# Mamba-2 inside a chunk: the values as weights, the decays moving, and a transpose back

## The chip, the cores and the metric

The kernel runs on one core of a Trainium2 chip. The metric is the device time of one execution in microseconds (us). TensorE (PE in the rows) multiplies, with its weight loads shown as an engine of their own (PEld); VectorE (DVE), ScalarE (ACT) and GpSimd (POOL) do the element-wise work; SyncE (SP) and ACT issue the DMAs.

## What is computed

One layer of a bidirectional encoder over 1024 tokens: a norm, one wide input projection, three recurrent branches (RWKV-7, HGRN2 and Mamba-2, called SSD), their gated sum, an output projection and an FFN. The change lies in the SSD branch. Cut to what matters, for each chunk of 128 tokens, 16 heads of 64 values, 2 groups of 8 heads:

```python
cb = jnp.einsum('bcqgn,bcsgn->bcqsg', cm, bm)
y_diag = jnp.einsum('bcqsgh,bcsghp->bcqghp', cb[..., None] * lmat, xdt)   # inside a chunk
...
y_off = jnp.einsum('bcqgn,bcghpn->bcqghp', cm, prev) * jnp.exp(a_cum)[..., None]
return (y_diag + y_off).reshape(b, L, H, P)
y = y_f + y_b + xs * d_skip[:, None]          # both directions and the skip
```

`y_diag` is the part in question: a 128x128 matrix per head and chunk (decays times scores) against 128x64 values.

## The kernel before

Everything is one instruction stream per engine. A scheduler that simulates the kernel sets the order on PE, DVE, ACT and SP; only POOL's order in the chunk loop is written by hand (`manual_schedule`). Products in full float32 run as two passes, so that eight matmuls show as 16 records; the wide products use float32r and one pass each.

`ssd` (L1204) handles the two groups of 8 heads one after the other. For a group it convolves the inputs (`conv`), transposes the values into token rows `xt` (L1347), and then runs the **chunk loop** (L1381), eight iterations. Iteration i works on chunk i in the forward direction (d=0) and on chunk 7-i in the backward one (d=1). In each direction:

- `yo` (L1391) multiplies by the state `S[d]`; DVE scales it to `yt` (L1393); POOL adds it to the accumulator `Y` (L1394).
- `xw` (L1397, DVE) and `st` (L1399, PE) give the state's update; POOL decays `S` (L1403), DVE adds (L1404; in the first iteration a copy, L1401).

`pairs(c)` (L1361) prepares the 128x128 matrices `E` of a later chunk: two DMAs broadcast the cumulated decays (L1367), POOL subtracts (L1370, twice), DVE picks the halves (L1373), ACT takes the exponential (L1374), DVE multiplies by the scores `CB` (L1375). The `E` buffers rotate, five in all. In iterations 0 to 3 POOL also starts two rows of `Y` from the skip (L1384).

At the end of iteration i stands the product `yd`: for each head, `E` as weights (128x128) and the head's 64 columns of `xt` moving, into one PSUM bank of token rows (128 x 512), which DVE adds to `Y[:, i]` (L1412).

Between these steps the kernel hands out **job matmuls**: the input projection of branches that come later, 3696 matmuls of 128x128 by 128x512 at L330 to L332, cut into pieces by `J.share` (L354). They keep PE busy while the chunk loop waits. Every job loads its weights (ACT cast `wh`, L221; DVE remainder `wl`, L223) and has its result copied out by ACT (`st`, L272) and stored. After the loop, `Y` is transposed into channel rows (`ytps`, L1430). When the second group is done, the branches are merged (`merges`, L1474), for which the last job results are loaded back (`gt`).

Of the kernel before, what the change touches and what calls it, by code (L numbers as in the profile page):

```python
# [9 lines left out]
F32 = mybir.dt.float32  # L10
# [8 lines left out]
P = 128  # L19
# [7 lines left out]
DECAY = 0.6065306597  # L27
NORM_EPS = 1e-6
EB = 5
TB = 6  # L30
PE = mybir.EngineType.PE
ACT = mybir.EngineType.Activation
# [967 lines left out]
def hgrn(g):  # L1000
# [3 lines left out]
    with ExitStack() as es:  # L1004
# [4 lines left out]
        def tl(tag, shape=(P, L), bufs=1, dt=F32):  # L1009
            return hp.tile(list(shape), dt, tag=tag, name=tag, bufs=bufs)  # L1010

        def gates(hd):

            kf = [tl("kf", bufs=2), tl("kb", bufs=2)]
            gg = tl("gg", bufs=2)
            sg = tl("t", bufs=TB)
            for d in range(2):
# [39 lines left out]
        def front(hd):  # L1057
# [4 lines left out]
            nc.sync.dma_start(fr.q, J.get(g.ph, hd))  # L1062
            lf = [tl("t", bufs=TB), tl("t", bufs=TB)]
            fr.cm = [tl("cf"), tl("cb")]
# [13 lines left out]
            fr.scd = tl("scd", (P, NT, 64))  # L1078
            ks = tl("t", bufs=TB)
            nc.vector.tensor_add(ks, kf[0], kf[1])  # L1080
# [11 lines left out]
        for hd in range(4):  # L1092
            fr = nxt
            q, gg, cm, scd = fr.q, fr.gg, fr.cm, fr.scd
            iv = tl("t", bufs=TB)
            nc.sync.dma_start(iv, J.get(g.ph, 12 + hd))
            Vt = tl("Vt", (P, NT, P))

            def transp(dst, src):
                for h in range(2):  # L1100
                    ps = pp.tile([P, 4, P], F32, tag="a", name="tps", bufs=4)
                    for j in range(4):
                        t = h * 4 + j
                        nc.tensor.transpose(ps[:, j], src[:, t * P:(t + 1) * P], g.ident)
                    nc.scalar.copy(dst[:, h * 4:h * 4 + 4], ps)
# [14 lines left out]
            for d in range(2):  # L1120
                c3, ck3 = (t.rearrange("p (c t) -> p c t", t=P) for t in (cm[d], fr.ck[d]))
                last = (P - 1) if d == 0 else 0
                kd = tl("t", bufs=TB)
                kd3 = kd.rearrange("p (c t) -> p c t", t=P)
# [5 lines left out]
            for d in range(2):  # L1130
                kt = tl("t", (P, NT, P), bufs=TB)
                transp(kt, kds[d])
# [71 lines left out]
def ssd(g, xr):  # L1204
    nc, tc, A, J = g.nc, g.tc, g.A, g.J
# [7 lines left out]
    with ExitStack() as es:  # L1213
        kp = es.enter_context(tc.tile_pool(name="s0", bufs=1))
        pp = es.enter_context(tc.tile_pool(name="s0ps", bufs=1, space=PSUM))
# [13 lines left out]
        with tc.tile_pool(name="s0t", bufs=1) as tp:  # L1229
# [15 lines left out]
            for src, dst in ((dt, dtT), (dA, dAT)):  # L1245
                ps = pp.tile([P, NT, 32], F32, tag="a", name="dtps", bufs=3)
# [43 lines left out]
        def conv(ct, dst):  # L1290

            pt = sp.tile([P, L + 4], F32, tag="E", name="pt", bufs=EB)
            nc.gpsimd.memset(pt[:, 0:2], 0.0)
            nc.gpsimd.memset(pt[:, L + 2:L + 4], 0.0)
            nc.sync.dma_start(pt[:, 2:L + 2], J.get(g.px, ct))
            w = V["conv_w"]
            acc = sp.tile([P, L + 4], F32, tag="E", name="acc", bufs=EB)[:, :L]
            nc.scalar.activation(acc, pt[:, 0:L], AF.Identity, scale=w[:, ct:ct + 1], bias=V["conv_b"][:, ct:ct + 1])
            for k in range(1, 5):
                nc.vector.scalar_tensor_tensor(acc, pt[:, k:k + L], w[:, k * 12 + ct:k * 12 + ct + 1], acc,  # L1300
                                               MUL, ADD)
            nc.scalar.activation(dst, acc, AF.Silu)
# [3 lines left out]
        yp = es.enter_context(tc.tile_pool(name="s1y", bufs=1))  # L1306
        sp = es.enter_context(tc.tile_pool(name="s1", bufs=1))
        for grp in range(2):
            with ExitStack() as es2:
                xt = ep.tile([P, NT, 512], F32, tag="xt", name="xt")  # L1310
# [9 lines left out]
                for h in range(2):  # L1320
                    ps = pp.tile([P, 4, P], F32, tag="a", name="cbps", bufs=3)
# [17 lines left out]
                for q in range(4):  # L1339
                    xq = sp.tile([P, L + 4], F32, tag="E", name="xq", bufs=EB)[:, :L]  # L1340
                    conv(grp * 4 + q, xq)
                    J.share(F[2])
                    for h in range(2):
                        ps = pp.tile([P, 4, P], F32, tag="a", name="xps", bufs=3)
# [5 lines left out]
                Y = yp.tile([P, NT, 512], F32, tag="Y", name="Y")  # L1350

                def per_head(tab, c, d):
                    return tab[:, c, d * 16 + grp * 8:d * 16 + grp * 8 + 8].unsqueeze(2).broadcast_to([P, 8, 64])

                def h3(t):
                    return t.rearrange("p (h v) -> p h v", v=64)
# [4 lines left out]
                def pairs(c):  # L1361

                    Es = []
                    for d in range(2):
                        e = sp.tile([P, L + 4], F32, tag="E", name="E", bufs=EB)
                        e = e[:, :L].rearrange("p (h t) -> p h t", t=P)
                        nc.sync.dma_start(e, cumd[d * 16 + grp * 8:d * 16 + grp * 8 + 8, c * P:(c + 1) * P]  # L1367
                                          .unsqueeze(0).broadcast_to([P, 8, P]))
                        cs = cums[:, c, d * 16 + grp * 8:d * 16 + grp * 8 + 8]
                        nc.gpsimd.tensor_tensor(e, e, cs.unsqueeze(2).broadcast_to([P, 8, P]), SUB)  # L1370
                        Es.append(e)
                    e = Es[0]
                    nc.vector.copy_predicated(e, m8.unsqueeze(1).broadcast_to([P, 8, P]), Es[1])  # L1373
                    nc.scalar.activation(e, e, AF.Exp)  # L1374
                    nc.vector.tensor_mul(e, e, CB[:, c:c + 1, :].broadcast_to([P, 8, P]))  # L1375
                    return e
# [4 lines left out]
                for i in range(NT):  # L1381
                    if i < NT // 2:
                        for c in (i, NT - 1 - i):
                            nc.gpsimd.tensor_tensor(h3(Y[:, c]), h3(xt[:, c]),  # L1384
                                                    gd[:, c].unsqueeze(2).broadcast_to([P, 8, 64]), MUL)
                    e = nxt.pop(0)
                    for d in range(2):
                        c = i if d == 0 else NT - 1 - i
                        if i > 0:
                            ps = pp.tile([P, 512], F32, tag="b", name="yo", bufs=2)  # L1390
                            nc.tensor.matmul(ps, CT[:, c * P:(c + 1) * P], S[d], start=True, stop=True)  # L1391
                            yt = yp.tile([P, 512], F32, tag="yt", name="yt", bufs=2)
                            nc.vector.tensor_tensor(h3(yt), h3(ps), per_head(ecum, c, d), MUL)  # L1393
                            nc.gpsimd.tensor_add(Y[:, c], Y[:, c], yt)  # L1394
                        if i < NT - 1:
                            xw = yp.tile([P, 512], F32, tag="xw", name="xw", bufs=2)
                            nc.vector.tensor_tensor(h3(xw), h3(xt[:, c]), per_head(wst, c, d), MUL)  # L1397
                            ps = pp.tile([P, 512], F32, tag="b", name="st", bufs=2)
                            nc.tensor.matmul(ps, Bt[:, c], xw, start=True, stop=True)  # L1399
                            if i == 0:  # L1400
                                nc.vector.tensor_copy(S[d], ps)  # L1401
                            else:
                                nc.gpsimd.tensor_tensor(h3(S[d]), h3(S[d]), per_head(dec, c, d), MUL)  # L1403
                                nc.vector.tensor_add(S[d], S[d], ps)  # L1404
                        if d == 0 and i + 2 < NT:
                            nxt.append(pairs(i + 2))
                        J.share(F[4])
                    ps = pp.tile([P, 8, 64], F32, tag="a", name="yd", bufs=3)
                    for h in range(8):
                        nc.tensor.matmul(ps[:, h], e[:, h], xt[:, i, h * 64:h * 64 + 64],  # L1410
                                         start=True, stop=True)
                    nc.vector.tensor_add(Y[:, i], Y[:, i], ps.rearrange("p h v -> p (h v)"))  # L1412
                    J.share(F[5])
                order.close()
                if grp == 1:
                    xr.load(*range(4))
                zss = []
                for q in range(4):
                    zs = sp.tile([P, L + 4], F32, tag="E", name="zs", bufs=EB)[:, :L]
                    nc.sync.dma_start(zs, J.get(g.pz, grp * 4 + q))  # L1420
# [4 lines left out]
                for q in range(4):  # L1425
                    zs = zss[q]
                    for h in range(2):
                        ps = pp.tile([P, 4, P], F32, tag="a", name="ytps", bufs=3)
# [7 lines left out]
                    else:  # L1436
                        sq = sp.tile([P, L + 4], F32, tag="E", name="sq", bufs=EB)[:, :L]
                        nc.scalar.activation(sq, zs, AF.Square)
# [593 lines left out]
def layer_kernel(ctx, tc, A, out):  # L2032
# [27 lines left out]
    g.gtp = ctx.enter_context(tc.tile_pool(name="gtp", bufs=1))  # L2060
    xr = Operand(g, r, (0,))
    ysc, ss = ssd(g, xr)
    rg = ExitStack()
    ring = [rg.enter_context(tc.tile_pool(name=f"ring{i}", bufs=1)) for i in range(2)]
# [72 lines left out]
```

## Time and profile before

| | |
|---|---|
| time, median of 3 runs | 2425.1 us (2421.72 to 2426.01) |
| the profiled execution | 2419.83 us, its span 2418.1 us |
| PE busy | 2276.5 us, 94% |
| DVE, POOL, ACT busy | 1568.5 (65%), 1041.6 (43%), 988.8 us (41%) |
| mean granted PE clock | 0.972 of 2.4 GHz |
| first and last product `yd` | 1139.8 and 1416.1 us from the span's start |
| `yd`, matmul records | 256, 35.8 us busy |

PE is busy nearly throughout, but this is an average. The two chunk loops lie at about 1137 to 1226 us and 1321 to 1422 us. In them POOL is busy 73.6 of 89 us and 77.6 of 101 us, against 43% over the span, and PE has its longest gaps there; between them, from 1226 to 1321 us, PE has none.

### The profile page before, as it was taken

The numbers are of one execution on the slowest core, as the hardware profiler recorded it, in microseconds if no ns is written. First come the engines' busy times: TensorE is split into PE (matmuls) and PEld (weight loads), VectorE is DVE, ScalarE is ACT, GpSimd is POOL, SyncE is SP. The second block draws the span as 40 slices with busy tenths as digits, with TensorE's granted clock in tenths as the row PEclk, the third lists the DMA queues.
The fourth block names the chain that finished last, engine by engine and source line by source line (L and its number), as shares of the span: only waits on it lengthen the run. The fifth ranks groups of instructions, "written<-read, shape, count | busy, mean of one in ns | idle before, by whom it ended". The sixth has DMA issues, their size and how long they took to land.

```text
span 2418.1 us, 37438 instructions
## 1 busy us (share of the span) xinstructions
PE 2276.5 (94%) x14785; PEld 1839.9 (76%) x14785; DVE 1568.5 (65%) x2041; ACT 988.8 (41%) x1436; POOL 1041.6 (43%) x817
## 2 busy tenths in 40 slices
PE   8998999999998998999999889999899999999895
PEld 6776778888777877887778667888688888877674
DVE  5678764456458568545756776442864554479999
ACT  6554532222456655435134154332433333344333
POOL 4433331443125335202841841430554444457985
PEclk9999999999999999999999999999999999999998
DMA  5455784764442232245545556531222222344211
GB/s 151 120 140 136 176 207 116 223 190 138 139 153 93 87 118 79 73 163 145 137 155 145 128 196 193 169 123 61 70 96 88 83 84 79 101 162 132 93 53 70
DMA packets 381213, 306.23 MB, mean 127 GB/s; under 512 B 111274, under 2 KB 323150, under 8 KB 381038
## 3 DMA queue, kind: packets, MB, share of 16 engines
q1 hardware_dynamic: 260909, 225.71, 31.5%
q10 hardware_dynamic: 119936, 77.61, 11.1%
q8 instruction: 116, 1.90, 0.3%
q0 software_dynamic: 192, 0.52, 0.1%
q14 instruction: 60, 0.48, 0.1%
HBM read 209.68 MB, written 94.11 MB: 126 GB/s over the span
## 4 chain that ended last, share of the span: by engine, by line
PE 62%; DVE 20%; POOL 5%; DMA 4%; issue 4%; ACT 3%; SPq 0%; ACTq 0%; DVEq 0%; POOLq 0%
PE mm L330 7%; PE mm L332 7%; PE mm L331 7%; PE ps L1589 6%; PE ps L1591 6%; PE ps L1590 6%; DVE ab L1806 3%; DVE acc L1928 2%; PE mm L231 2%; PE mm L232 2%; PE mm L233 2%; POOL E L1370 2%; DMA E<-cumd 2%; DVE rb L1806 1%; PE Gps L807 1%
## 5 line engine op out<-in xcount | busy, mean ns | idle before, releaser
L330 PE MATMUL mm<-x,wh 128*128 128x512 f32 (+1 forms) x1232 | 500.9, 407 | 0.6 <-ACT wh L221 0.5
L331 PE MATMUL mm<-x,wh 128*128 128x512 f32 (+1 forms) x1232 | 492.5, 400 | 0.0
L332 PE MATMUL mm<-x,wl 128*128 128x512 f32 (+1 forms) x1232 | 489.7, 398 | 0.1
L330 PEld LDWEIGHTS mm<-x,wh 128*128 128x128 f32 (+1 forms) x1232 | 232.6, 189 | 62.2 <-issue 10.4
L332 PEld LDWEIGHTS mm<-x,wl 128*128 128x128 f32 (+1 forms) x1232 | 232.9, 189 | 54.8 <-issue 4.6
L331 PEld LDWEIGHTS mm<-x,wh 128*128 128x128 f32 (+1 forms) x1232 | 233.2, 189 | 53.9 <-issue 7.1
L1591 PE MATMUL ps<-xb,rb 128*128 128x512 f32 x432 | 168.1, 389 | 0.0
L1590 PE MATMUL ps<-xb,rb 128*128 128x512 f32 x432 | 168.1, 389 | 0.0
L1589 PE MATMUL ps<-xb,rb 128*128 128x512 f32 x432 | 168.0, 389 | 0.0
L221 ACT CAST wh<-wr 128x1024 fp32r<-128x1024 f32 (+2 forms) x103 | 100.2, 973 | 110.3 <-PE mm L331 89.6
L1589 PE MATMUL ps<-rb,ab 128*128 128x512 f32 x308 | 125.6, 408 | 19.6 <-DVE acc L1928 18.7
L223 POOL TENSOR_TENSOR wl<-wr,wh 128x1024 fp32r<-128x1024 f32 x30 | 79.1, 2638 | 134.8 <-ACT wh L221 113.1
L1590 PE MATMUL ps<-rb,ab 128*128 128x512 f32 x308 | 122.7, 398 | 2.9 <-POOL rb L1806 2.9
L223 DVE TENSOR_TENSOR wl<-wr,wh 128x1024 fp32r<-128x1024 f32 (+2 forms) x73 | 95.2, 1304 | 44.6 <-ACT wh L221 44.5
L1591 PE MATMUL ps<-rb,ab 128*128 128x512 f32 x308 | 121.3, 396 | 1.5 <-DVE ab L1806 1.5
L1753 ACT CAST rb<-fs 128x512 fp32r<-128x512 f32 x85 | 52.6, 622 | 167.3 <-PE ps L1591 117.7
L272 ACT COPY st<-mm 128x512 f32<-128x512 f32 x130 | 75.5, 582 | 98.2 <-PE mm L332 82.3
L1370 POOL TENSOR_TENSOR E<-E,cums 128x1024 f32<-128x1024 f32 x32 | 70.4, 2211 | 61.6 <-DMA E<-cumd 61.6
L810 DVE TENSOR_TENSOR Gc<-Gps,mk 128x256 f32<-128x256 f32 x64 | 27.2, 425 | 107.4 <-PE Gps L807 61.7
L231 PE MATMUL mm<-oh,wh 128*128 128x512 f32 x224 | 89.4, 403 | 6.4 <-DVE gt L1493 4.3
L1928 DVE TENSOR_TENSOR acc<-acc,ps 128x512 f32<-128x512 f32 x148 | 94.1, 674 | 0.0
L1590 PEld LDWEIGHTS ps<-xb,rb 128*128 128x128 f32 x432 | 81.1, 188 | 17.0
(504 smaller groups left out, 5400.4 us busy)
## 6 DMA issues: line engine op xcount, KB each, us to landing
wr<-in_w_in_dram ACTq DMA_DIRECT2D x74, 512.0 KB
fr<-in_ffn_w_in_dram SPq DMA_DIRECT2D x44, 512.0 KB
E<-cumd SPq DMA_DIRECT2D x32, 512.0 KB
pg<-st ACTq DMA_DIRECT2D x48, 256.0 KB
gt<-pg SPq DMA_DIRECT2D x24, 512.0 KB
ad<-a SPq DMA_DIRECT2D x22, 512.0 KB
dr<-in_ffn_w_down_dram SPq DMA_DIRECT2D x22, 512.0 KB
ar<-ad SPq DMA_DIRECT2D x22, 512.0 KB
```

The costliest lines, as they stand in the source:

```text
L221: nc.scalar.copy(hi[:, :kt, :n], raw[:, :kt, :n])
L223: g.lo_eng.tensor_sub(lo[:, :kt, :n], raw[:, :kt, :n], f32(hi[:, :kt, :n]))
L231: nc.tensor.matmul(ps, whi[:, k, :n], xh, start=(k == 0), stop=False)
L330: g.nc.tensor.matmul(ps[:n], w[0][:, k, :n], xh, start=(k == 0), stop=False)
L331: g.nc.tensor.matmul(ps[:n], w[0][:, k, :n], xl, start=False, stop=False)
L332: g.nc.tensor.matmul(ps[:n], w[1][:, k, :n], xh, start=False, stop=(k == KT - 1))
L1370: nc.gpsimd.tensor_tensor(e, e, cs.unsqueeze(2).broadcast_to([P, 8, P]), SUB)
L1589: nc.tensor.matmul(ps, ah, bh, start=(i == 0), stop=False)
L1590: nc.tensor.matmul(ps, ah, bl, start=False, stop=False)
L1591: nc.tensor.matmul(ps, al, bh, start=False, stop=(i == n - 1))
L1806: eng.tensor_sub(blk[:, 1], s, f32(blk[:, 0]))
L1928: nc.vector.tensor_add(m[j], m[j], ps)
```

## The change

In the product inside a chunk the operands change sides. Before, `E` of a head was the weights and 64 value columns moved; now the 64 value columns are the weights (128x64) and `E` moves (128 columns). The result has values on partitions and tokens in columns. Even heads write partitions 0 to 63 and odd heads 64 to 127 of a bank, so that the bank holds four 128x128 blocks of two heads each. ACT copies the bank to SBUF (`yf`, one buffer), PE transposes its four blocks into a second bank (`ydt`, from the same three PSUM buffers), and DVE adds that to `Y`. The piece of jobs at `F[5]` now stands between the copy and the transposes.

```diff
+YF = 1
...
-                    ps = pp.tile([P, 8, 64], F32, tag="a", name="yd", bufs=3)
+
+                    ps = pp.tile([P, 4, P], F32, tag="a", name="yd", bufs=3)
                     for h in range(8):
-                        nc.tensor.matmul(ps[:, h], e[:, h], xt[:, i, h * 64:h * 64 + 64],
+                        nc.tensor.matmul(ps[h % 2 * 64:h % 2 * 64 + 64, h // 2], xt[:, i, h * 64:h * 64 + 64], e[:, h],
                                          start=True, stop=True)
-                    nc.vector.tensor_add(Y[:, i], Y[:, i], ps.rearrange("p h v -> p (h v)"))
+                    yf = yp.tile([P, 4, P], F32, tag="yf", name="yf", bufs=YF)
+                    nc.scalar.copy(yf, ps)
                     J.share(F[5])
+                    ps = pp.tile([P, 4, P], F32, tag="a", name="ydt", bufs=3)
+                    for q in range(4):
+                        nc.tensor.transpose(ps[:, q], yf[:, q], g.ident)
+                    nc.vector.tensor_add(Y[:, i], Y[:, i], ps.rearrange("p q v -> p (q v)"))
```

The changed kernel has one more line from L30 on and seven more after the loop, so L1391 is L1392 there, L330 is L331, and so on. Only 128 matmuls change and 64 are added, but the scheduler orders the work around them anew.

The first place is PE early in the first chunk loop. Before (the rest of chunk 1's product, all of chunk 2's, with `yo` and `st` of the state between them; mm are job matmuls):

```order
L332 MATMUL mm<-x_382,wl 128x512
L1410 MATMUL yd<-xt,E 128x64 x5
L1391 MATMUL yo<-S_10630,CT 128x512
L1410 MATMUL yd<-xt,E 128x64 x9
L1399 MATMUL st<-xw,Bt 128x512
L1410 MATMUL yd<-xt,E 128x64 x2
L330 MATMUL mm<-x_391,wh 128x512
```

Now, at the same place:

```order
L331 MATMUL mm<-x_400,wh 128x512
L1419 MATMUL ydt<-ident,yf 128x128 x4
L1412 MATMUL yd<-E,xt 64x128
L1392 MATMUL yo<-S_10630,CT 128x512
L1412 MATMUL yd<-E,xt 64x128 x7
L332 MATMUL mm<-x_401,wh 128x512
L333 MATMUL mm<-x_400,wl 128x512
L331 MATMUL mm<-x_409,wh 128x512
L332 MATMUL mm<-x_410,wh 128x512
L333 MATMUL mm<-x_409,wl 128x512
L1400 MATMUL st<-xw,Bt 128x512
```

Chunk 1's product is cut once, with a full-width `yo` inside it, and chunk 2's product no longer follows at once: 18 job matmuls now come first.

The second place is DVE in the third iteration of the first loop, from the choice of halves (COPY_PREDICATED) for chunk 3 to the add of a product to `Y`. Before:

```order
L1373 COPY_PREDICATED E<-m_10190,E 128x1024
L1397 TENSOR_TENSOR xw<-xt,wst 128x512
L1404 TENSOR_TENSOR S_10630<-S_10630,st 128x512
L1375 TENSOR_TENSOR E<-E,CB 128x1024
L1393 TENSOR_TENSOR yt<-yo,ecum 128x512
L1412 TENSOR_TENSOR Y<-Y,yd 128x512
```

Now:

```order
L1374 COPY_PREDICATED E<-m_10190,E 128x1024
L1398 TENSOR_TENSOR xw<-xt,wst 128x512
L1405 TENSOR_TENSOR S_10630<-S_10630,st 128x512
L1376 TENSOR_TENSOR E<-E,CB 128x1024
L224 TENSOR_TENSOR wl<-wr,wh 128x1024
L1394 TENSOR_TENSOR yt<-yo,ecum 128x512
L1420 TENSOR_TENSOR Y<-Y,ydt 128x512
```

A job's `wl` has moved ahead of `yt`; the add to `Y` keeps its place behind `yt`, and here belongs to an earlier chunk than before.

## Rows read from the trace of the kernel before

**Rows 1.** Stretches: busy per engine PE, PEld, DVE, ACT, POOL; clock; DMA share; GB/s

```profile
1137.00:1226.00 89.00, 79.89 (x336) 57.76 (x336) 65.10 (x60) 22.12 (x25) 73.63 (x43) 0.92 0.58 153
1226.00:1321.00 95.00, 95.00 (x463) 78.68 (x462) 54.10 (x54) 39.76 (x53) 19.16 (x23) 1.00 0.51 151
1321.00:1422.00 101.00, 87.26 (x370) 61.39 (x368) 74.10 (x70) 24.73 (x28) 77.60 (x47) 0.95 0.56 137
```

**Rows 2.** Chain that ended last, one iteration of the first loop: start, us, what

```profile
1207.41 1.52 DVE xw L1397
1208.93 0.60 DVE S L1404
1209.53 1.14 DVE E L1375
1210.67 0.61 DVE yt L1393
...
1213.63 5.15 POOL E L1370 x2
```

**Rows 3.** Waits in the first loop: us in total, times, longest

```profile
POOL Y L1394 <- DVE yt L1393: 17.4, 7, 4.2
...
DVE Y L1412 <- POOL Y L1394: 8.8, 6, 1.6
...
PE yd L1410 <- DVE E L1375: 1.8, 2, 1.1
...
ACT E L1374 <- DVE E L1373: 52.8, 7, 11.6
```

**Rows 4.** Timeline: a product yd of eight heads, second loop: start, us, what

```profile
1329.46 1.89 PE L1410 MATMUL yd<-xt,E 128*128 128x64 f32 x16
```

**Rows 5.** Timeline: half-array products of other branches among job matmuls

```profile
1028.73 0.39 PE L330 MATMUL mm<-x,wh 128*128 128x512 f32 x1
1029.05 1.15 PE L1053 MATMUL vps<-lv 128*64 128x64 f32 x32
...
1030.47 0.39 PE L332 MATMUL mm<-x,wl 128*128 128x512 f32 x1
...
560.93 1.16 PE L807 MATMUL Gps<-ARc,BKc 64*128 64x128 f32 x16
```

**Rows 6.** Weight loads and passes: duration min/median/max in ns, first and last start

```profile
L1410 PEld LDWEIGHTS yd<-xt,E x256: 186/192/338, 1139.8 to 1416.1; 128*128 128x128 f32 x128
L1410 PE MATMUL yd<-xt,E x256: 217/275/476, 1140.0 to 1416.2; 128*128 128x64 f32 x128
...
L1053 PEld LDWEIGHTS vps<-lv x896: 132/138/232, 745.6 to 1029.9; 128*64 128x64 f32 x180
L1053 PE MATMUL vps<-lv x896: 222/222/369, 745.6 to 1030.0; 128*64 128x64 f32 x180
```

**Rows 7.** Timeline: twelve 128x128 transposes among job matmuls

```profile
1108.31 0.39 PE L330 MATMUL mm<-x,wh 128*128 128x512 f32 x1
1108.54 0.60 PE L1326 MATMUL btps<-ident,BT 128*128 128x128 f32 x4
1108.98 1.04 PE L1347 MATMUL xps<-ident,xq 128*128 128x128 f32 x8
...
1110.08 0.39 PE L332 MATMUL mm<-x,wl 128*128 128x512 f32 x1
```

**Rows 8.** Timeline: ACT's copy of a 128x512 PSUM bank

```profile
1156.41 0.57 ACT L272 COPY st<-mm 128x512 f32<-128x512 f32 x1
```

**Rows 9.** Stretches early in the first loop, columns as in rows 1

```profile
1155.00:1160.00 5.00, 2.88 (x17) 2.12 (x15) 4.40 (x5) 1.53 (x2) 4.56 (x3) 0.93 0.61 161
1160.00:1165.00 5.00, 5.00 (x18) 3.97 (x18) 2.85 (x4) 0.00 (x0) 5.00 (x4) 0.50 0.58 174
```

**Rows 10.** Timeline: POOL and PE waits at the second loop's start

```profile
1340.14 1.90 POOL L1370 TENSOR_TENSOR E<-E,cums 128x1024 f32<-128x1024 f32 x1 [5.19 <-DMA E<-cumd]
...
1336.18 0.66 PE L1410 MATMUL yd<-xt,E 128*128 128x64 f32 x2 [4.83 <-DVE E L1375]
```

## Prediction

> **What bounds the kernel now.** I read the share of busy time first, then cut the span into stretches around the change [rows 1], then followed the chain that ended last through one of them [rows 2], and last looked at who waits for whom there [rows 3]. The stretches show three regimes. Between the two chunk loops PE is busy 95.00 of 95 us: there PE sets the pace, by the number of job matmuls that are left. In the loops PE has 9.1 and 13.7 us of gaps, and POOL is busy 73.6 of 89 and 77.6 of 101 us. The chain says what leads in a loop [rows 2]: DVE does xw, S, E and yt (1.52 + 0.60 + 1.14 + 0.61), then POOL adds yt to Y, decays S and does two E (5.15 for these), and DVE starts over with the E that POOL has just finished. PE isn't in this ring. POOL waits for DVE's yt 17.4 us in seven waits of the first loop; PE waits for E only 1.8 us there [rows 3]. So in the loops an edit counts if it delays DVE or POOL in this ring, and PE's work counts only where PE loses the lead over it. All of the change lies in the loops.
>
> **PE's own work.** Before: eight products of a chunk are 16 passes in 1.89 us [rows 4]; less the last pass's own 0.275 us [rows 6] that is, over 15 steps, 0.108 us from pass to pass, 1.72 us a chunk, 27.6 us for 16 chunks. Only 64 columns move in such a pass, and the weights are 128 wide; their load takes 192 ns where a 64 wide load takes 138 [rows 6], so 64 columns more or less are 54 ns, and 128 columns are just the 0.108 us. The load sets this pace.
>
> Now: 64 columns of weights, 128 columns moving, and neighbouring heads on different halves of the array. The trace of before has no such shape. The nearest are products on half the array's columns with 64 columns moving, 32 passes in 1.15 us, and products on half of its rows with 128 columns moving, 16 passes in 1.16 us [rows 5]. With a last pass of 0.222 us [rows 6] and, for the second, yd's 0.275, they stand 0.030 and 0.059 us apart. Both show two halves at work at once, for a pass alone with 64 moving columns would need the 54 ns. I take 0.059, since 128 columns move: 0.94 us a chunk, 15.1 us in all. The bounds are 0.030 (7.7 us) and 0.108, no overlap at all (27.6 us).
>
> Changing between whole and half array costs something on its own. From the job matmul at 1028.73 to the second after the block, at 1030.47, are 1.74 us [rows 5]; two job matmuls' steps are 0.46 (0.23 each, as from 1108.31 to 1108.54 [rows 7]) and 32 passes 0.96, so going in and out costs about 0.33 us. The scheduler cuts the products by yo and st, which use the whole array: I count 17 half-array stretches in the first loop and 13 in the second, 30 x 0.33 = 9.9 us.
>
> The Trainium skill, TensorE: Matmul & The Clock Gate, Part 3 (The mechanism), says that a weight load overlaps with a running matmul only when the two are in different row groups. Here both halves use all rows, so by that rule loads and products would stand one behind the other, which is the second rival below. The rows of half-column products at 0.030 us, less than one 54 ns load, speak against it.
>
> Transposes: twelve of them between job matmuls take 1110.08 - 1108.31 - 0.46 = 1.31 us [rows 7], 0.110 each; 64 of them are 7.0 us. So PE goes from 27.6 to 15.1 + 9.9 + 7.0 = 32.0 us, **4.4 us more work, not less**: 2.9 in the first loop (17 x 0.33 + 7.55 + 3.5 - 13.8), 1.5 in the second (with 13).
>
> **What that does on the path.** In the first loop PE gets more lead than it loses. Today chunk 2's products stand right behind chunk 1's, and PE waits for E there: of 1155 to 1160 us it is busy 2.88 us, and then the granted clock is 0.50 (1.2 GHz) from 1160 to 1165 [rows 9], which costs some 2.1 + 2.5 = 4.6 us. In the new order 18 job matmuls stand between, so this second wait should be covered. An earlier wait, of chunk 0's yo for the first S, stays, since yo stands where it stood. A lead of 4.6 less 2.9 us: PE doesn't hold the ring up, and the surplus turns into waits at later yo and st. In the second loop 1.5 us fall into 13.7 us of gaps. So PE's sum counts only behind the ring: after the last chunk of the first loop, where PE takes over, stand one job matmul more (387 for 386 to the next loop's first product, 0.23) and the extra of two half-done chunks (2 x 0.44 for transposes, 2 x 0.33, less 0.78 on the products): +1.0 us.
>
> At both loops' starts PE is on the path in another way: chunk 0's products free a buffer of E, whose next DMA POOL waits for (5.19 us [rows 10]). They shrink from 1.72 to 0.94 + 0.33: -0.45 us twice, -0.9 us.
>
> **The copy on ACT** is 16 x 0.57 = 9.1 us [rows 8]. ACT is busy 22 and 25 us in the loops [rows 1] and waits 52.8 us in seven waits ahead of the exponential [rows 3], 7.5 us each. In the order the copy stands ahead of the next exponential, and the products that it needs are through before it, so it fills idle time. If it came late, it would hold the exponential and with it the ring: the third rival.
>
> **DVE's add** stays one instruction of the same size, in the same slot behind yt, now up to an iteration after its product. There it used to wait for POOL's Y 8.8 us in six waits [rows 3], 1.5 each. The new condition, four transposes (0.44 us) after a yo that PE issues in front of them, should be met within that wait. What moves the ring is the order ahead of yt: in each loop one add (0.6) leaves that place and one comes there in a later iteration, and a job's wl, which I price like E's 1.14 us [rows 2], comes there once in the first loop. Sum 0 to +1.1; two of these fall into iterations 2 and 3, where POOL also has two L1384 to do, so I take +0.5.
>
> **Sum:** +1.0 - 0.9 + 0.5 = **+0.6 us**. The profiled execution took 2419.83 us, 1.73 more than its span, and 5.3 less than the median of the runs. The edits are sized on that execution; on the median it gives 2425.1 + 0.6 = 2425.7 us. 0.2% (4.85 us), about what a measurement can tell from no change, is far more than this.
>
> **Rivals.**
> 1. *PE leads after all, and the saved wait counts.* If PE's lag after the stall is what paces the first loop, its 4.6 - 2.9 = 1.7 us come through. At the second loop's start PE waits 4.83 us for E [rows 10]; now 16 job matmuls (3.6 us) stand ahead of chunk 1's products, which would cover 3.6 us and perhaps 2.5 us of low clock behind it as in rows 9, less 1.5. Together -1.7 - 4.6 = -6.3 us: 2418.8. For it: PE is busy 79.9 of 89 us of the first loop [rows 1], so it is never far from the lead. Against it: POOL waits for DVE, not for PE. Chance 0.18.
> 2. *No overlap of the halves.* The products stay at 0.108 us, PE has 12.5 us more. First loop 2.9 + 6.3 - 4.6 = +4.6 beyond the lead, second loop 1.5 + 6.3 in 13.7 us of gaps, of which perhaps a third shows (+2.6): with the +0.6, 2432.9. Against it: rows 5. Chance 0.08.
> 3. *A new wait in the ring* (slower). ACT and DVE work in order. If PE reaches a chunk's products late, the copy waits at ACT's head and the next exponential behind it; or the transposes come later than POOL's Y, and DVE's add holds S and the next yt. Each would add about the copy and one transpose set, 0.6 to 1.0 us, to the 12 iterations that the ring leads: +7 to +12, 2434. It decides when the transposes end more than 1.5 us after yt. For it: the scheduler places them to be ready just in time, by a simulation. Against it: 7.5 us of slack ahead of each exponential. Chance 0.15.
>
> **How the numbers follow.** My forecast has 0.59 and a range of its own from 2421.5 to 2430 (pass bounds, half-array changes, DVE order). Of rival 1 most is faster by over 0.2% (0.16), with 0.03 from the forecast's tail: 0.19. Rival 3, most of rival 2 and a tail of 0.05: 0.25 slower. The rest, 0.56, is within 0.2%. To leave out no more than 2 in 10 the range goes from 2418.5, just under rival 1's time, to 2433.5, short of rival 3's.
>
> **What would show it.** The products' 16 passes should take about 1.15 us where they aren't cut, at 0.059 us; 0.108 would be rival 2. The gap at 1155 to 1160 us and the low clock behind it should be gone, and POOL's waits for yt still be there at about 17 us. DVE's add should wait for POOL or hardly at all; if it waits for the transposes, or the exponential for the copy, rival 3 holds. If POOL waits longer at the loops' starts for the DMA of E, my -0.9 is wrong. A loop that is shorter by 3 us or more, with POOL's waits down, would prove rival 1.

## The result, and the profile after

The changed kernel takes 2427.35 us in the median (2423.2 to 2434.08, 18 runs), beside 2422.16 us for the kernel before (2417.3 to 2426.95, 18 runs): a ratio of 1.0019, with a 95% interval of 1.0012 to 1.0026, so +2.9 to +6.3 us. A second comparison, below, gives 1.0012 (1.0002 to 1.0023). The profiled execution took 2423.20 us, with a span of 2421.5 us; before, 2419.83 and 2418.1. It is the quickest of its 18, 4.2 us under their median (before, 2.3 under), so the two traces hold 3.4 us of the 4.6 by which the ratio 1.0019 sets the kernels apart. The question is where these 3.4 us of span arise.

The stretches of [rows 1] in the changed kernel: busy us and instructions of PE, PEld, DVE, ACT, POOL; then granted clock, DMA share, GB/s.

```profile
1137.00:1226.00 89.00, 78.47 (x366) 50.82 (x364) 64.46 (x60) 25.71 (x33) 72.11 (x42) 0.96 0.65 152
1226.00:1321.00 95.00, 95.00 (x467) 77.89 (x467) 55.03 (x54) 40.77 (x53) 18.13 (x23) 1.00 0.49 149
1321.00:1422.00 101.00, 90.81 (x404) 58.30 (x402) 75.81 (x70) 30.76 (x38) 80.88 (x48) 0.92 0.54 144
```

They look much like before. ACT has the copies (22.12 to 25.71 and 24.73 to 30.76 us), PE holds more instructions and still has gaps of 10.5 and 10.2 us in the loops. Its mean granted clock moved both ways: from 0.92 to 0.96 in the first loop, from 0.95 to 0.92 in the second.

PE's timeline in the changed kernel (start, us, what): a job matmul and behind it an uncut block of eight products, 16 passes; two waits; a second uncut block, and the second job matmul behind it.

```profile
1140.06 0.39 PE L333 MATMUL mm<-x,wl 128*128 128x512 f32 x1
1140.38 1.10 PE L1412 MATMUL yd<-E,xt 128*64 128x128 f32 x16
...
1155.85 1.13 PE L1392 MATMUL yo<-S,CT 128*128 128x512 f32 x2 [0.80 <-DVE yt L1394]
...
1160.53 1.13 PE L1400 MATMUL st<-xw,Bt 128*128 128x512 f32 x2 [1.18 <-DVE S L1405]
...
1186.14 1.09 PE L1412 MATMUL yd<-E,xt 128*64 128x128 f32 x16
...
1187.50 0.39 PE L331 MATMUL mm<-x,wh 128*128 128x512 f32 x1
```

With a last pass of 0.273 us (its row below) the passes stand (1.10 - 0.273) / 15 = 0.055 us apart, where [rows 4] gave 0.108. Both ends of a block cost something on top. From the job matmul at 1140.06 to the first pass are 0.32 us, where a job takes 0.23: 0.09 for the way into the half-array form. From the first pass at 1186.14 to the second job matmul behind the block are 1.36 us: 0.88 for the passes, 0.23 for a job, and 0.25 for the way out.

The passes of the products, and the copies on ACT, by tile: duration min/median/max in ns, first and last start.

```profile
L1412 PE MATMUL yd<-E,xt x256: 272/273/476, 1140.4 to 1412.9; 128*64 128x128 f32 x128
...
L1415 ACT COPY yf<-yd x16: 566/586/589, 1147.3 to 1415.6; 128x512 f32<-128x512 f32 x16
```

The waits of the first loop in the changed kernel (us in total, times, longest), over the stretch of [rows 3], 1130 to 1240 us:

```profile
ACT E L1375 <- DVE E L1374: 44.4, 8, 7.6
POOL Y L1395 <- DVE yt L1394: 20.1, 7, 4.2
...
DVE Y L1420 <- POOL Y L1395: 5.6, 4, 1.4
...
PE yd L1412 <- DVE E L1376: 0.4, 1, 0.4
```

Against [rows 3]: the products hardly wait for E any more (1.8 to 0.4 us), DVE's add waits less for POOL (8.8 to 5.6 us), and POOL's waits for yt are still there, at 20.1 us for 17.4. All eight exponentials wait for DVE's choice of halves, none for a copy. The second stall of [rows 9] reads now

```profile
1155.00:1160.00 5.00, 3.56 (x22) 2.01 (x21) 4.07 (x5) 2.12 (x3) 5.00 (x4) 1.00 0.67 167
1160.00:1165.00 5.00, 4.47 (x17) 3.12 (x17) 3.18 (x4) 0.00 (x0) 5.00 (x4) 1.00 0.55 178
```

in the same columns: PE is busy 3.56 and 4.47 us where it was 2.88 and 5.00, and the granted clock stays at 1.00 (2.4 GHz) where it fell to 0.50 (1.2 GHz). In the kernel before, the gap of 2.12 us was two waits of PE, and only the second was for E:

```profile
1156.64 1.12 PE L1391 MATMUL yo<-S,CT 128*128 128x512 f32 x2 [1.05 <-DVE yt L1393]
...
1159.45 2.82 PE L1410 MATMUL yd<-xt,E 128*128 128x64 f32 x12 [1.07 <-DVE E L1375]
```

The one for E is gone, the one for yt is 0.80 us, and one for S (1.18, at 1160.53) is new. So the gaps of these ten us are 1.97 us for 2.12: what is saved here is the low clock, hardly the wait.

**Where the 3.4 us are.** I cut each span at two marks: the first pass of yd, and the last product with the operand `or` in the merges that follow the loops, at helper line L232 (L231 in the kernel before and in those made from it). These rows give the second marks, before and then changed:

```profile
L231 PE MATMUL mm<-or,wh x32: 389/389/389, 1534.2 to 1616.4; 128*128 128x512 f32 x32
```

```profile
L232 PE MATMUL mm<-or,wh x32: 389/390/390, 1534.5 to 1616.8; 128*128 128x512 f32 x32
```

From mark to mark, both loops and the merges, are 1616.8 - 1140.4 = 476.4 us; before, 1616.4 - 1140.0 [rows 6], the same 476.4. From the second mark to the end are 804.7 us; before, 801.7. (The last 0.4 us stand ahead of the first mark.) So the loops, where the edit is, cost nothing, and the loss lies far behind them. From mark to mark, in the columns of [rows 1], before and then changed:

```profile
1140.00:1616.40 476.40, 443.48 (x1950) 345.01 (x1949) 302.95 (x301) 167.13 (x196) 222.35 (x146) 0.96 0.54 157
```

```profile
1140.40:1616.80 476.40, 445.17 (x2015) 334.50 (x2015) 306.81 (x302) 176.08 (x212) 221.29 (x145) 0.96 0.54 157
```

At the same mean clock PE is busy 1.7 us longer, and its gaps are 1.7 us shorter (31.2 for 32.9). The first and last of the FFN's products with xb and rb, before and then changed, bound the loss further:

```profile
L1589 PE MATMUL ps<-xb,rb x432: 388/389/389, 1709.9 to 2144.9; 128*128 128x512 f32 x144
```

```profile
L1596 PE MATMUL ps<-xb,rb x432: 388/390/390, 1710.2 to 2148.0; 128*128 128x512 f32 x144
```

Behind the second mark the first stands at 93.5 and 93.4 us, the last at 528.5 and 531.2: 2.7 of the 3.0 us arise in between. It is here, at the start of the FFN. VectorE's timeline, first before, then after (xb: remainders of the FFN's input; gb and rb: remainders of weights):

```profile
1741.71 1.28 DVE L1639 TENSOR_TENSOR xb<-xr,xb 128x512 fp32r<-128x512 f32 x2
1742.92 0.67 DVE L1784 TENSOR_TENSOR c<-c,ps 128x512 f32<-128x512 f32 x1
1743.51 2.88 DVE L1754 TENSOR_TENSOR gb<-fr,gb 128x512 fp32r<-128x512 f32 x2
```

```profile
1742.59 1.40 DVE L1646 TENSOR_TENSOR xb<-xr,xb 128x512 fp32r<-128x512 f32 x1
1743.91 3.48 DVE L1761 TENSOR_TENSOR gb<-fr,gb 128x512 fp32r<-128x512 f32 x2
1747.32 1.74 DVE L1646 TENSOR_TENSOR xb<-xr,xb 128x512 fp32r<-128x512 f32 x1
```

and PE in the changed kernel behind that:

```profile
1749.12 0.50 PE L1597 MATMUL ps<-xb,gb 128*128 128x512 f32 x1 [2.25 <-DVE xb L1646]
```

No line of the FFN was edited. The scheduler places instructions by times that it works out for the whole program; with other work in the loops it put VectorE's last xb behind two gb instead of ahead of them. The program text there is the same, the order isn't.

### The profile page after: what moved, and what is told of

Same layout as the page of the kernel before. It is cut to its first block, busy times and chain, and to the rows that moved or that the text cites. A ratio compares the mean times of both kernels' runs of the same rounds, so it can differ in the third digit from the quotient of the medians.

```text
span 2421.5 us, 37580 instructions
## 1 busy us (share of the span) xinstructions
PE 2279.0 (94%) x14849; PEld 1831.9 (76%) x14849; DVE 1574.0 (65%) x2041; ACT 997.1 (41%) x1452; POOL 1038.5 (43%) x817
## 5 line engine op out<-in xcount | busy, mean ns | idle before, releaser
L331 PE MATMUL mm<-x,wh 128*128 128x512 f32 (+1 forms) x1232 | 500.5, 406 | 0.6 <-ACT wh L222 0.5
L331 PEld LDWEIGHTS mm<-x,wh 128*128 128x128 f32 (+1 forms) x1232 | 233.6, 190 | 62.7 <-issue 11.3
L1596 PE MATMUL ps<-rb,ab 128*128 128x512 f32 x308 | 126.0, 409 | 20.1 <-DVE acc L1935 18.0
L224 DVE TENSOR_TENSOR wl<-wr,wh 128x1024 fp32r<-128x1024 f32 (+2 forms) x73 | 100.6, 1378 | 53.5 <-ACT wh L222 53.2
L232 PE MATMUL mm<-oh,wh 128*128 128x512 f32 x224 | 88.9, 401 | 5.5 <-DVE gt L1500 4.2
```

Source lines behind the costliest of these rows:

```text
L224: g.lo_eng.tensor_sub(lo[:, :kt, :n], raw[:, :kt, :n], f32(hi[:, :kt, :n]))
L232: nc.tensor.matmul(ps, whi[:, k, :n], xh, start=(k == 0), stop=False)
L331: g.nc.tensor.matmul(ps[:n], w[0][:, k, :n], xh, start=(k == 0), stop=False)
L1596: nc.tensor.matmul(ps, ah, bh, start=(i == 0), stop=False)
```

## Experiments

The ratios are to the kernel before, run on the same chip in the same job; us are that ratio times 2421. Theories, as the expectations use them: **A**, mine, says that in the loops a ring of VectorE and POOL leads and TensorE's work is hidden, so that the loops cost next to nothing and the wait in the FFN makes up the rest; **B**, that the loops cost the 4.6 us; C and D came later. All kernels but e2_behind and after_again carry the edit of e1_ahead, so that the last xb stands ahead of the gb in them. In the diffs `issue_behind(a, b)` stands for a dependency that sets only the order of issue of two instructions on one engine.

**1. The FFN's order alone, both ways.** The changed kernel with the last xb put ahead of the first gb on ScalarE and VectorE, and of the sum c on VectorE:

```diff
+            if f == 1 and j == 1:
+                issue_behind(hi, self.x.lasta)
+                issue_behind(lo, self.x.last)
...
                 elif j == 6:
-                    nc.vector.tensor_add(c, c, ps)
+                    add = nc.vector.tensor_add(c, c, ps)
+                    if f == 0:
+                        issue_behind(add, self.x.last)
```

> The changed kernel with one more edit: at the start of the FFN, the last remainder of the FFN's input (xb) is put ahead of the two weight remainders gb in VectorE's and ScalarE's order, as it stands in the kernel before. The chunk loops are exactly those of the changed kernel. Theory A (the loops cost nearly nothing, +0.3 us; the rest of the +3.4 us between the two profiled executions is TensorE's 2.25 us wait for that remainder): 2.2 to 3.5 us under the changed kernel, so 0 to +2 us against the kernel before (ratio 1.000 to 1.0008), and no wait of TensorE for xb over 1 us behind 1745 us. Theory B (the loops cost the 4.6 us, and the FFN's wait would have been hidden by what comes later): the ratio stays at 1.0012 to 1.0026.

Measured: 0.9998 (0.9989 to 1.0007), span 2417.8 us. Mark to mark 476.7, rest 801.4 us, as in the kernel before (476.4 and 801.7). PE's longest wait for xb at the FFN's start is 1.5 us.

The kernel before with the last xb put behind the second gb (`late` and `second` are their instructions on the two engines):

```diff
-            self.split(4, raw[k][:, 1])
+            if k < 3:
+                self.split(4, raw[k][:, 1])
+        self.rest = lambda: self.split(4, raw[3][:, 1])
...
                 self.w.pump()
+                if f == 0 and j == 7:
+                    self.x.rest()
+                    for late, second in zip(self.x.last, self.second):
+                        issue_behind(late, second)
```

> The kernel before with the same edit the other way round: the last remainder xb is put behind the two weight remainders gb at the FFN's start; the chunk loops are those of the kernel before. Theory A: a wait of TensorE for xb of 2 to 4 us near 1747 us, and the kernel 2.2 to 4 us slower than before (ratio 1.0009 to 1.0017), without any change of the products. Theory B: within 1 us of the kernel before, since TensorE makes the wait up later.

Measured: 1.0008 (1.0000 to 1.0017), just under what A expected, span 2420.9. Mark to mark 476.1, rest 803.9 us, and in PE's timeline the wait is there without any change of the products:

```profile
1747.64 0.50 PE L1590 MATMUL ps<-xb,gb 128*128 128x512 f32 x1 [1.74 <-DVE xb L1638]
```

The changed kernel once more, in another job:

> The changed kernel once more, unedited, beside the next three on one chip. By the 18 runs so far it should be 1.0012 to 1.0026 of the kernel before, some 4 to 5 us more than e1_ahead. In the trace, TensorE's wait for the last remainder xb near 1749 us should be there again at about 2.2 us, and the second merge product should end as far behind the loops' first product as in the kernel before, to 1 us.

Measured: 1.0012 (1.0002 to 1.0023), span 2421.3; mark to mark 475.9, rest 804.4 us. The rest of the span is 801.4 to 802.1 us in every kernel up to e7 that has the last xb ahead, and 803.9 to 804.7 in the three that have it behind. B falls: it is this order, at 2.2 to 3.3 us of span.

**2. TensorE's work in the loops: hidden or not?** The products with neighbours on the same half:

```diff
-                    for h in range(8):
+                    for h in (0, 2, 4, 6, 1, 3, 5, 7):
```

> The kernel of e1_ahead with the eight products in the order 0, 2, 4, 6, 1, 3, 5, 7, so that neighbours use the same half of the array's columns. If the halves overlap because neighbours lie on different halves, the 16 passes take 1.7 to 2.0 us instead of 1.10, some 0.6 to 0.9 us more for each of 16 chunks, 10 to 14 us of TensorE's time. Theory A (TensorE's work in the loops is hidden behind the ring of VectorE and POOL, and counts only for the two half-done chunks behind the first loop and the loops' starts): +1 to +4 us on e1_ahead. Rival (TensorE leads in the loops): +8 to +14 us.

Measured: 1.0009 (0.9999 to 1.0020), 2.7 us over e1_ahead by the ratios; mark to mark 481.0, 4.3 us more. An uncut block in PE's timeline:

```profile
1190.11 1.58 PE L1412 MATMUL yd<-E,xt 128*64 128x128 f32 x16
```

That is 0.087 us from pass to pass instead of 0.055: alternating halves gains 0.48 us a chunk, 7.7 us in all, less than I had expected. By the marks about half of that reaches the end, by the ratios a third; the profiled execution lies 4.7 us over the median of its runs. That is inside A's 1 to 4 us or just above them, and the next run spoke against A.

The products issued twice:

```diff
-                    for h in range(8):
+                    for h in (*range(8), *range(8)):
```

> The kernel of e1_ahead with the eight products of a chunk issued twice into the same bank: 16 passes at 0.055 us more for each of 16 chunks, 14 us of TensorE's work and nothing else. Theory A: since 7.7 us more (e3_same_half) cost 2 to 4 us, 14 us cost 3 to 8 us, the more so as the gaps of the loops, 10 us in each, fill up. Rival (TensorE leads): +13 to +15 us.

Measured: 1.0099 (1.0085 to 1.0113), 24 us more than e1_ahead for 16 x (1.97 - 1.10) = 13.9 us of work; mark to mark 498.3, 21.6 more. Part of it is a new wait, since the scheduler again changed an order. Timelines of ACT, DVE and PE near the second loop's end:

```profile
1416.51 1.06 ACT L1428 ACTIVATE zs<-zs 128x1024 f32<-128x1024 f32 x1 [7.10 <-DMA zs<-pz]
```

```profile
1418.53 1.22 DVE L224 TENSOR_TENSOR wl<-wr,wh 128x1024 fp32r<-128x1024 f32 x1 [8.23 <-ACT wh L222]
```

```profile
1421.00 2.07 PE L1400 MATMUL st<-xw,Bt 128*128 128x512 f32 x2 [6.91 <-DVE S L1405]
```

ACT's zs, which waits for its DMA, now stands ahead of a job's cast; DVE's remainder of that job waits for the cast, S stands behind it on DVE, and PE waits for S. This takes 6.9 of the 21.6 us; the other 14.7 are about the 13.9 us of added work. The job matmuls alone (their tile x), from the last product to the second mark (PE busy and count, clock, DMA share, GB/s):

```profile
1442.90:1643.60 200.70, 14.01 (x58) 1.00 0.54 180
```

In e1_ahead none stand there. The loops could not hold these 58, and they were done behind them, 14.0 us of PE's time. This is theory **D**: the end is TensorE's own work plus its waits, and work put into the loops pushes job matmuls out of them.

The transposes left out (part of the result stays in columns):

```diff
-                    for q in range(4):
-                        nc.tensor.transpose(ps[:, q], yf[:, q], g.ident)
-                    nc.vector.tensor_add(Y[:, i], Y[:, i], ps.rearrange("p q v -> p (q v)"))
+                    nc.vector.tensor_add(Y[:, i], Y[:, i], yf.rearrange("p q v -> p (q v)"))
```

> The kernel of e1_ahead without the 64 transposes: VectorE adds the copied products as they are, so this part of the result is left in columns. It takes 7.0 us of TensorE's work out of the loops and one step between the copy and VectorE's add. Theory A (TensorE's work is hidden there but for the two half-done chunks behind the first loop): 0 to 2 us less than e1_ahead. Rival (TensorE leads): 5 to 7 us less.

Measured: 1.0026 (1.0012 to 1.0040), 6.8 us slower than e1_ahead with 7 us less to do on TensorE. It decides nothing between A and D, because VectorE's add now reads SBUF twice instead of SBUF and PSUM, and holds `yf`, which has one buffer, until it is done: ACT's copies wait 35.2 us for it, in eight waits. By tile, the add of the changed kernel and of this one (min/median/max ns):

```profile
L1420 DVE TENSOR_TENSOR Y<-Y,ydt x16: 666/683/689, 1160.4 to 1421.5; 128x512 f32<-128x512 f32 x16
```

```profile
L1417 DVE TENSOR_TENSOR Y<-Y,yf x16: 677/1515/2379, 1156.4 to 1432.4; 128x512 f32<-128x512 f32 x16
```

Sixteen adds at a median of 1.5 us in place of 0.68 are some 13 us on VectorE, and the transposes, which bring the sum into PSUM, avoid just that.

**3. The ring of VectorE and POOL.** The copy on VectorE:

```diff
-                    nc.scalar.copy(yf, ps)
+                    nc.vector.tensor_copy(yf, ps)
```

> The kernel of e1_ahead with the copy of the products out of PSUM on VectorE instead of ScalarE. Theory A (VectorE and POOL are the ring that leads in the loops; ScalarE has room): 16 copies of 0.6 to 0.65 us enter the ring in some 12 iterations, +5 to +9 us on e1_ahead. Rival (VectorE isn't on the path, its copies fall into its own waits for POOL): within 2 us of e1_ahead.

Measured: 0.9997 (0.9988 to 1.0006), mark to mark 477.4: no slower than e1_ahead. 16 copies of 0.68 us are 10.8 us on VectorE, and its waits gave way. Waits of DVE over both loops, e1_ahead, then this one:

```profile
DVE E L1374 <- POOL E L1371: 28.8, 13, 7.2
...
DVE Y L1420 <- POOL Y L1395: 9.2, 7, 1.5
```

```profile
DVE E L1374 <- POOL E L1371: 25.8, 12, 5.9
...
DVE Y L1420 <- POOL Y L1395: 5.0, 4, 1.4
```

Of the 10.8 us 7.2 come out of these two; DVE's waits for POOL's decay of S grew by 3.9 (8.2 to 12.1), so where the rest went isn't shown. But the end did not move. So a VectorE instruction in the loops isn't on the path for being there; A falls here too.

The sum of yt into Y on VectorE instead of POOL:

```diff
-                            nc.gpsimd.tensor_add(Y[:, c], Y[:, c], yt)
+                            nc.vector.tensor_add(Y[:, c], Y[:, c], yt)
```

> The kernel of e1_ahead with the sum of yt into Y on VectorE instead of POOL, 28 times. POOL loses 28 x 1.27 = 35 us of work and its waits for yt (36 us over both loops); VectorE gets 28 x 0.67 = 19 us more. Theory C, formed after e4_copy_dve cost nothing (POOL, which works in order and waits for yt, is what leads in the loops, and VectorE only by the step between POOL's E and yt): the loops get 5 to 15 us shorter, ratio 0.994 to 0.998. Theory A as I had it (VectorE leads as much as POOL): +0 to +10 us.

Measured: 0.9987 (0.9978 to 0.9995), span 2416.1; mark to mark 472.5, 4.2 us less than e1_ahead. It is faster than both kernels, by 3 us than the kernel before and by 6 to 8 us than the changed one, and POOL no longer stands between yt and the next E. The gain is smaller than theory C wanted (5 to 15 us). Whether the kernel before would gain as much from it wasn't tried.

**4. TensorE in program order.** To keep the scheduler from moving things, the program sets TensorE's order in the loops:

```diff
-                order.enter_context(tc.manual_schedule(engines={POOL}))
+                order.enter_context(tc.manual_schedule(engines={POOL, PE}))
```

> The kernel of e1_ahead with TensorE's order in the chunk loops set by the program, as POOL's is, so that the scheduler no longer cuts a chunk's eight products by yo and st: 16 half-array stretches instead of 30. Theory D, formed after e6_twice (the end is TensorE's own work plus its waits; its work counts in full, in the loops too, since a job matmul that finds no room in the loops is done behind them): 14 changes fewer at the 0.35 us that the changed kernel's trace shows are 4.9 us less, with the loops' waits (22 to 27 us so far) open to both sides: 10 us less to 3 us more than e1_ahead, likeliest 4 us less. Theory A (TensorE's work hidden): no gain from the changes, within 2 us but for the waits.

Measured: 1.0243 (1.0229 to 1.0257), far outside all that was expected. Most of the loss stands ahead of the loops, in the stretch from 1000 to 1123 us, where PE was busy 122.26 us before:

```profile
1000.00:1123.00 123.00, 74.76 (x544) 61.06 (x543) 75.19 (x82) 50.99 (x65) 23.77 (x28) 0.75 0.30 90
```

Job matmuls that used to fill that stretch were now held in the loops by their place in the program, and PE lost 47.5 us there. So the run says nothing on the 14 changes of form that it saves. But it makes a frame in which an edit moves little else. With the sum on VectorE in it (the edit of e7_sum_dve):

> e9_order and e7_sum_dve together: TensorE in program order, and the sum of yt into Y on VectorE. If both gains add up, 7 to 8 us under the kernel before (ratio 0.9965 to 0.9975); if both take away the same waits, no better than the better of the two.

Measured: 1.0244 (1.0230 to 1.0258): the sum on VectorE brings nothing in this frame. With the products twice in it (the edit of e6_twice):

> e9_order with the eight products of a chunk issued twice into the same bank: 14 us more of TensorE's work, and since the program sets TensorE's and POOL's order, nearly no other instruction moves (which e6_twice could not keep). Theory D: 11 to 15 us more than e9_order. Theory A: 2 to 6 us more.

Measured: 1.0330 (1.0316 to 1.0344), 21 us more than e9_order for 13.9 us of work; mark to mark 570.3 against 552.4 us, 17.9 more: PE is busy 13.5 us longer at the same mean clock (0.96), and its gaps are 4.4 us longer. D said 11 to 15, A said 2 to 6: TensorE's work counts in full and some waits grow on top of it.

The products of the kernel before in the same frame:

```diff
--- before
-                order.enter_context(tc.manual_schedule(engines={POOL}))
+                order.enter_context(tc.manual_schedule(engines={POOL, PE}))
```

> The products of the kernel before (values moving, whole array, no copy, no transposes) under TensorE's program order, with the FFN's late remainder ahead as in e1_ahead: against e9_order only the change itself is left, without any new order around it. TensorE's work by the traces: before 16 x 1.72 = 27.5 us; changed, uncut, 16 x (0.88 + 0.35 + 0.46 to 0.53) = 27.0 to 28.2 us. So e9_order and this one should agree within 2 us, under theory A and D alike; a difference of 4 us and more would be a wait of the new chain copy, transposes, sum.

Measured: 1.0226 (1.0211 to 1.0242), mark to mark 547.7: in this frame the kernel before is faster than the changed one, by 4 us by the ratios, whose intervals overlap, and by 4.7 by the marks. Mark to mark, e9_order, then this one, in the columns of [rows 1]:

```profile
1123.50:1675.90 552.40, 514.59 (x2350) 395.77 (x2350) 318.67 (x308) 190.17 (x233) 223.31 (x145) 0.96 0.51 147
```

```profile
1124.80:1672.50 547.70, 514.92 (x2286) 404.14 (x2286) 317.65 (x308) 181.43 (x217) 222.80 (x145) 0.98 0.53 149
```

PE is busy equally long, at a lower clock in the changed one, and its gaps are 37.8 us there against 32.8. All waits of PE over the loops, e9_order, then this one (us in total, times, longest):

```profile
PE ydt L1419 <- ACT yf L1415: 20.7, 7, 9.9
PE st L1400 <- DVE S L1405: 3.2, 3, 2.3
PE yo L1392 <- DVE yt L1394: 1.7, 1, 1.7
```

```profile
PE st L1399 <- DVE S L1404: 9.0, 7, 3.3
PE yo L1391 <- DVE yt L1393: 5.8, 2, 5.0
PE st L1399 <- DVE S L1401: 5.6, 2, 4.4
```

With the transposes only nine job matmuls behind the products, PE waits 20.7 us for ACT's copy, and most of the other waits go: 25.6 us in all against 20.4. So the new chain does cost a wait where the transposes come too early. In the changed kernel itself the scheduler put them far enough back that they hardly ever wait (1.0 us, once, in the second loop).

## Why the prediction was right, and where it wasn't

I forecast 2425.7 us and within 0.2%; the median was 2427.35 us and the ratio 1.0019. The forecast holds, but the sum of +0.6 us is 2.3 us short of the interval's lower end, and it holds partly by luck: 2425.7 lies near 2427.35 also because it starts from the median of three runs, 2425.1, where 18 runs of the kernel before gave 2422.16. By its steps:

- **The step that failed: "All of the change lies in the loops."** Inside its frame the sum was good: mark to mark the change costs 0.0 us, and -0.5 in its second execution, against +0.6. Outside it, 2.2 to 3.3 us were lost by the new order at the FFN's start (e1_ahead, e2_behind). This could have been priced. The order showed one xb behind two gb, and the two take 2.88 us in the trace of before: a term of 0 to +2.9 us.
- **Passes:** 0.055 us measured, 0.059 forecast. The second rival, no overlap, is gone. The Trainium skill, TensorE: Matmul & The Clock Gate, Part 3 (The mechanism), which has weight loads overlap only between row groups, would give the alternating and the same-half order one time; e3_same_half shows 0.055 and 0.087 us, so here the column halves matter, and the measurement decides.
- **Changes of form and transposes: too dear.** 0.09 us in and 0.25 out round an uncut block are 0.34, against 0.33 forecast. But the kernel before, which has 30 blocks as well, pays for them too, and the sum left that out. An uncut one in e11_before_order, and the second job matmul behind it:

```profile
1124.84 1.90 PE L1410 MATMUL yd<-xt,E 128*128 128x64 f32 x16
...
1126.86 0.39 PE L331 MATMUL mm<-x,wh 128*128 128x512 f32 x1
```

These are 2.02 us, 0.07 more than 1.72 for the passes and 0.23 for a job. As an estimate from uncut blocks, 30 of them cost 30 x 0.27 = 8.1 us net, not 9.9, and TensorE's work goes up by 14.1 + 8.1 + 7.0 - 27.6 = 1.6 us, not 4.4. From mark to mark PE is busy 1.7 us longer.
- **The second stall:** the low clock behind it went as forecast. The gap did not (2.12 to 1.97 us): the forecast put all of it down to E, and half was a wait for yt.
- **"PE's sum counts only behind the ring": wrong.** e6_twice and e12_order_twice show TensorE's work counting in full, and e4_copy_dve shows 10.8 us more on VectorE costing nothing. What paid for PE's added work is not the saved low clock of the second stall either: the second loop lost about as much clock as the first gained (0.95 to 0.92, 0.92 to 0.96), and the mean from mark to mark is 0.96 in both kernels. In this execution PE's gaps shrank by as much as its busy time grew; in after_again they are 33.8 us, 0.9 more than before, at a mean clock of 0.97. So the -0.5 to 0.0 comes about in different ways, and that +0.6 lies near it is luck as much as reckoning. TensorE's work counting was the premise of the first rival, though its -6.3 us did not come.
- **The second loop's start:** as forecast, POOL got E's buffer earlier: its wait of 5.19 us [rows 10] became 2.52. PE's wait of 4.83 us for E went too, but three waits for S took its place, 5.84 us together, so neither my -0.45 nor the first rival's gain came through. PE's waits in the changed kernel there:

```profile
1334.33 1.74 PE L1392 MATMUL yo<-S,CT 128*128 128x512 f32 x2 [2.23 <-DVE S L1402]
1338.61 2.07 PE L1400 MATMUL st<-xw,Bt 128*128 128x512 f32 x2 [1.27 <-DVE S L1402]
1348.76 2.08 PE L1400 MATMUL st<-xw,Bt 128*128 128x512 f32 x2 [2.34 <-DVE S L1405]
```

- **The copy on ACT and DVE's add** fit into waits as forecast. The third rival stayed away. In e9_order there is a new wait for the copy, but it stands on PE and not in the ring of DVE and POOL.
- **DVE's order, +0.5 us:** nothing of it is seen. The end of the loops varies more than that from one execution to the next (the last sum into Y stands 282.7, 285.1 and 285.8 us behind the first mark in three kernels with the same loops), while mark to mark stays within 0.8 us (475.9 to 476.7).

What stays open: how much of TensorE's added work the waits take back. They took back 3.4 of 7.7 us in e3_same_half by the marks, 5.0 by the ratios, and none in e6_twice and e12_order_twice, and I have no rule for it from these runs.

## What to carry to other kernels

Where a scheduler orders the whole program by worked-out times, an edit in one place can move a late instruction in another: compare the orders to the end of the program, and price every instruction that moved ahead of something TensorE waits for. TensorE is busy 94% of the span here, and work added to it counted in full in two trials and by a third to a half in one; what the loops couldn't hold was done behind them. So count such an engine's work and its waits, and test by adding a known dose of work rather than by looking at who waits for whom. A small sum that comes out right isn't evidence for its terms.

## What the runs showed of the hardware that I had not expected

- Products on alternating column halves stand 0.055 us apart, on the same half 0.087 us, both with 64 wide weights and 128 columns moving. So even without alternation a pass costs less than the 0.108 us of the whole-array form.
- An add on VectorE with both operands in SBUF takes 0.68 to 2.38 us (median 1.5) beside POOL's work in these loops; with one operand in PSUM it stays at 0.67 to 0.69. In e7_sum_dve, where POOL no longer sums yt, 28 adds with both operands in SBUF take 0.68 to 2.38 us too, but with a median of 0.82. The Trainium skill, SBUF — State Buffer, section "SBUF: two separate sides", says that a VectorE instruction with two SBUF inputs and a GpSimd instruction that reads SBUF lock the same port pair for their whole duration. That agrees with these rows: bringing a summand through PSUM is worth some 0.8 us an add in e5_no_transpose, and less where POOL does less.
